# A hybrid encoder step: tokens normalized ahead of the input projection, convolutions that read PSUM, norms of queries and keys applied on load

## The chip, the cores and the metric

One core of a Trainium2 chip. The metric is the device time of one execution in microseconds. The engines are TensorE (PE, with PEld for its weight loads), VectorE (DVE), ScalarE (ACT), GpSimd (POOL) and SyncE (SP), which issues the DMAs.

## What is computed

One layer over 2048 prompt tokens (one request, zero states) and 8 x 16 sample tokens (with states), all in float32. Cut to what matters:

```python
h = rms_norm(x, norm_mix)                     # D_MODEL = 1024
p = h @ w_in                                  # 2056 columns GDN, 1824 columns RWKV
# gated delta rule: 4 heads of 128
qkv, gdn_conv_new = causal_dwconv(p_gdn[..., :1536], gdn_conv_buf, gdn_conv_w)   # 4 taps
q, k, v = split(silu(qkv))
q = l2_normalize(q) * 128 ** -0.5;  k = l2_normalize(k)
o_gdn, s_gdn_new = gdn_chunked(q, k, v, log_g, beta, s_gdn)
o_gdn = rms_norm(o_gdn, gdn_norm) * silu(z)
# RWKV-7: 8 heads of 64
ps, shift_new = causal_dwconv(p_rwkv, shift_buf, [rwkv_mu, 1 - rwkv_mu])         # 2 taps
kk = l2_normalize(kr * rwkv_k_k)
y, s_rwkv_new = rwkv7_recurrence(r, log_w, kr * (1 + (a - 1) * k_a), vr, -kk, kk * a, s_rwkv)
x = x + concat([o_gdn, o_rwkv]) @ w_out
# feed-forward of 2816 with a causal convolution of 3 taps in the gate
up = rms_norm(x, norm_ffn) @ w_up
gate, ffn_new = causal_dwconv(up[..., :2816], ffn_buf, ffn_conv_w)
x = x + (silu(gate) * up[..., 2816:]) @ w_down
y = rms_norm(x, norm_final)
```

The last rows before each convolution and the states are outputs too.

## The kernel before

Channels lie on partitions and tokens along the free dimension. The tokens go in five groups: 3, 4, 3, 3 blocks of 128, and 3 blocks with the 128 sample tokens behind them, so 384 or 512 columns. Each group has an input phase (`phase_in`) and an output phase (`phase_out`), in the order in0, in1, in2, out0, in3, out1, in4, out2, out3, out4.

Every projection is done in three passes (`mm3`): weight and input are each split into a rounded part and the rest (`split_w`, L419; `split_x`, L493). A block of 128 output channels is 24 products into one PSUM bank out of a ring of four (`psb`), which also serves the small products `psw`, `psa`, `psl`, `psbo`, `psgt` and `psn`. The scaling by 1/rms is left out of the inputs: the split takes x times the norm's weight, the sum of squares (`sumsq`) is made beside it, and 1/rms of each token (`g.rs`, tile `rsx`) is multiplied in as the bank is emptied.

That happens in `conv` (L506): POOL copies the history's last columns ahead of a tile `P` (L512), DVE writes bank times 1/rms into `P` (L513), POOL copies the new history out (L514), ACT multiplies with the last tap (L515), and DVE adds the other taps from shifted columns of `P` (L517). For the sample the same is done by segments (L521 to L527). The feed-forward's gate uses `conv` too.

`l2scale` (L616) runs four times per input phase, once for each GDN head and pair of RWKV heads. It sums squares on PE, takes Ln and Exp on ACT, stores the result to DRAM, loads it back spread over the partitions (`res<-l`, L632 and L635), multiplies q and k by it (L637) and stores them (`gd`). The direction of RWKV's keys waits for the same transfer (L764) before it is multiplied with the decays and stored (`rx`).

The two recurrences (`gdn_block` for 128 tokens and four heads, 17 of them; `rwkv_half` for 128 tokens and four heads, 34 of them) load these arrays (`gkq`, `rX`) and run beside the phases of other groups. Between their products stand long chains over DVE, ACT and POOL, with the inverse of triangular matrices (L788 to L837) the longest.

What sets the order: every part is a generator that yields the time its next operands are thought to take, and `drive` (L389) writes PE's order out from that, with the projections' products in the gaps of the recurrences. The order on the other engines comes from a planner that simulates the time. All DMAs are issued in order on SP's queue. The weights are loaded through four tiles `w32` and split by ACT (L425) and, by turns, POOL and DVE (L429).

Of the kernel before, what the change touches and what calls it, by code (L numbers as in the profile page):

```python
# [66 lines left out]
C_F32 = C_SI        # float32 up to here, masks behind  # L67
# [39 lines left out]
def pack_host(a):  # L107
    """Layout only: slices, transposes, zero padding."""
# [79 lines left out]
class Group:  # L188
    def __init__(self, t0, blocks, sample):
        self.t0, self.P, self.S = t0, blocks * 128, 128 if sample else 0  # L190
        self.nb, self.blk0 = blocks, t0 // 128
        self.n = self.P + self.S
        self.prep, self.tails, self.done, self.x = None, [], 0, None

    def seg(self, t):
        """the sample's part of a [p, tokens] AP, by request"""
        return t[:, self.P:self.n].rearrange("p (s t) -> p s t", t=SEG)


def bc(a, n):  # L200
    """a, along a new last axis"""
    return a.unsqueeze(len(a.shape)).to_broadcast(list(a.shape) + [n])


class Build:
# [7 lines left out]
    # ------------------------------------------------------------ set-up  # L213
    def setup(self, ctx):
# [14 lines left out]
        self.eps = cp.tile([128, 3], F32, name="eps")  # L229
        for i, v in enumerate((NEPS, LNEPS, 1.0)):  # L230
            nc.vector.memset(self.eps[:, i:i + 1], v)
# [32 lines left out]
        # constants by value  # L264
        self.mhalf = cp.tile([128, 1], F32, name="mhalf")
        nc.vector.memset(self.mhalf, -0.5)

        # parameters worked out once
# [8 lines left out]
        self.cw = der("cw", q("cw"), 0.5, own=True)           # half the taps: silu(y) = (1 + tanh(y/2)) y/2  # L277
# [6 lines left out]
        self.nhgn = der("nhgn", q("gn"), -0.5)  # L284
# [11 lines left out]
        # conv histories, and the sample's  # L296
# [12 lines left out]
        # per-token and per-block scalars  # L309
# [7 lines left out]
        # states: minus GDN's, and RWKV's with keys on partitions  # L317
# [4 lines left out]
        self.SB = [cp.tile([128, 2, 2, 64], F32, name=f"SB{i}") for i in range(2)]      # by pairs of heads, block-diagonal  # L322
# [3 lines left out]
        # scratch  # L326
        for i, g in enumerate(self.groups):
            d = lambda n, s: self.dp.tile(s, F32, name=f"{n}{i}")
            g.gd = d("gd", [4, 4, 128, g.n])        # k q v z, by head
            g.rx = [d(f"rx{j}_", [5, 128, g.n]) for j in range(4)]  # L330
            g.rh = d("rh", [8, 128, g.n])
            g.l2 = [d(f"l2{j}_", [6, g.n]) for j in range(4)]
# [6 lines left out]
    def a(self, g, name, dt=F32):  # L339
        """of the ring that the feed-forward's activations have in their phase"""  # L340
# [48 lines left out]
    def drive(self, main):  # L389
        """main to its end, then what is left of the tasks"""  # L390
# [18 lines left out]
    def load_w(self, src, tiles=KT):  # L409
        """[128, tiles * 128] of a weight, by [128, 512]"""  # L410
# [8 lines left out]
    def split_w(self, src, tiles=KT, ws=None):  # L419
        """a weight as pairs of [128, 512]: rounded, and what is left"""  # L420
# [12 lines left out]
    def mm3(self, ps, w, xs):  # L433
        """ps = sum over tiles of w^T x, both split: three passes"""
# [10 lines left out]
    def load_tok(self, g, t, a):  # L445
        """a group's tokens from [128, all tokens] of DRAM"""
# [9 lines left out]
    def pow_(self, out, in_):  # L456
        sh = list(in_.shape)
        e = self.mhalf
# [13 lines left out]
    def rms(self, g, acc):  # L472
        """in place: 1/rms of the channels whose squares acc sums by partition, on every partition"""
# [11 lines left out]
    def rsqrt(self, out, ps, scale=1.0):  # L485
        """(scale ps + eps)^-1/2"""
# [6 lines left out]
    def split_x(self, g, x, w=None):  # L493
        """x, times w of each channel: rounded, and what is left"""
# [10 lines left out]
    # ------------------------------------------------------------ causal convolution of a projected tile  # L505
    def conv(self, g, ps, rs, taps, hist, samp, out, rows=128):  # L506
# [4 lines left out]
        P = self.tp_.tile([128, 3 + 512], F32, tag="P", name="P", bufs=2)  # L511
        nc.gpsimd.tensor_copy(P[:, 0:h], hist)  # L512
        nc.vector.tensor_tensor(P[:, h:h + g.P], ps[:, 0:g.P], rs[:, 0:g.P], MUL)  # L513
        nc.gpsimd.tensor_copy(hist, P[:, g.P:g.P + h])  # L514
        nc.scalar.mul(out[r, 0:g.P], P[r, h:h + g.P], taps[-1][r])  # L515
        for i in range(h - 1, -1, -1):
            nc.vector.scalar_tensor_tensor(out[r, 0:g.P], P[r, i:i + g.P], taps[i][r], out[r, 0:g.P], op0=MUL, op1=ADD)  # L517
        S = None
        if g.S:
            S = self.tp_.tile([128, SEGS, 3 + SEG], F32, tag="PS", name="PS", bufs=1)  # L520
            nc.gpsimd.tensor_copy(S[:, :, 0:h], samp)  # L521
            nc.vector.tensor_tensor(S[:, :, h:h + SEG], g.seg(ps), g.seg(rs), MUL)
            nc.gpsimd.tensor_copy(samp, S[:, :, SEG:SEG + h])
            o = g.seg(out)
            nc.scalar.mul(o[r], S[r, :, h:h + SEG], taps[-1][r])
            for i in range(h - 1, -1, -1):
                nc.vector.scalar_tensor_tensor(o[r], S[r, :, i:i + SEG], taps[i][r], o[r], op0=MUL, op1=ADD)  # L527
        return P, S

    def shift(self, g, ps, i, out, rows=128):  # L530
        return self.conv(g, ps, g.rs, [self.q("mu")[:, i:i + 1], self.omu[:, i:i + 1]], self.hs[:, i:i + 1], self.ss[:, i, :].unsqueeze(2), out, rows)
# [4 lines left out]
    # ------------------------------------------------------------ input projection and all that is per token  # L536
    def phase_in(self, g):
        nc, q = self.nc, self.q
        xs = []
        g.rs = self.acc(g)  # L540
        ld = g.x or [self.load_x(g, k) for k in range(KT)]
        for k in range(KT):
            xs.append(self.split_x(g, ld[k], q("nm")[:, k:k + 1]))
            self.sumsq(g, g.rs, ld[k], k == 0)
        norm = self.spawn(self.late_rms(g, g.rs, 12000))
# [9 lines left out]
        # low-rank inputs  # L555
# [5 lines left out]
        self.shift(g, low[0], 0, la)  # L561
        nc.scalar.activation(la[0:64], la[0:64], AF.Tanh)
        sga = self.a(g, "sga")
        self.shift(g, low[1], 1, sga)
# [3 lines left out]
        P, S = self.shift(g, low[2], 2, sgb, 32)  # L568
        nc.scalar.activation(sgb[0:32], sgb[0:32], AF.Tanh, scale=0.5)
        nc.vector.tensor_scalar(sgb[0:32], sgb[0:32], 0.5, 0.5, op0=MUL, op1=ADD)  # L570
        self.spawn(self.gates(g, P, S))

        left = []
        for j in range(4):
            qk = []
            for a in range(2):
                ps = yield from block(15 + 4 * j + a)
                qk.append(self.prep_gdn(g, j, a, ps))
            left.append(self.spawn((yield from self.prep_rwkv(g, j, block, la, sga, sgb, qk))))
            for a in range(2, 4):  # L580
                ps = yield from block(15 + 4 * j + a)
                self.prep_gdn(g, j, a, ps)
        g.prep = left

    def gates(self, g, P, S):
        """beta and log decay of each token and GDN head, tokens on partitions"""
# [5 lines left out]
        for b in range(g.nb):  # L592
            self.tr(ps[:, 8 * b:8 * b + 8], P[64:72, 1 + 128 * b:129 + 128 * b], idn)
        if g.S:
            sm = self.t(g, "gth")[:, 0:128]
            nc.scalar.copy(sm[64:72].rearrange("p (s t) -> p s t", t=SEG), S[64:72, :, 1:17])
            self.tr(ps[:, 8 * g.nb:8 * g.nb + 8], sm[64:72], idn)
# [18 lines left out]
    def l2scale(self, g, j, qk, kk):  # L616
        """(sum of squares over a head's channels + eps)^-1/2 of RWKV's keys, GDN's queries and keys: the sums
        side by side in the array, 32 rows each, and the results spread over the partitions through DRAM"""
        nc = self.nc
        yield LB  # L620
        ps = self.psb(g, "psl")
        ss = (kk["s"], qk[0][1], qk[1][1])
        for n, s in enumerate(ss):
# [3 lines left out]
        nc.scalar.activation(rs[0:96], ps[0:96], AF.Ln, bias=self.eps[0:96, 0:1])  # L627
        nc.scalar.activation(rs[0:96], rs[0:96], AF.Exp, scale=-0.5)
        self.store(g.l2[j], rs[0:96:16])
        rk, rq, rK = [self.t(g, "res", 8) for _ in range(3)]  # L630
        for n in range(2):
            nc.sync.dma_start(rk[64 * n:64 * n + 64], g.l2[j][n:n + 1].to_broadcast([64, g.n]))  # L632
        kk["r"] = rk
        for n, r in enumerate((rq, rK)):
            nc.sync.dma_start(r, g.l2[j][2 + 2 * n:3 + 2 * n].to_broadcast([128, g.n]))  # L635
            y = qk[n][0]
# [677 lines left out]
```

## Time and profile before

| | |
|---|---|
| time of three runs | 3560.24, 3566.49, 3572.14 us |
| span of the profiled execution | 3558.0 us |
| PE, DVE, ACT, POOL busy | 95%, 67%, 42%, 52% |
| mean granted TensorE clock | 0.972 |
| DMA | 447.58 MB, mean 126 GB/s |

Of the profiled execution only the span from its first to its last instruction is known; it is 2.2 us under the fastest of the runs and 8.5 under their median. An engine's busy time counts its instructions, not the waits of its queue. A row of a group gives the line, engine, operation, out<-in, shapes and count, then busy time and mean ns of one, then the engine's idle time just before them and what ended it. A row of the timeline gives start and length in us and, in brackets, the idle time before it. A row of stretches gives the stretch, the busy time and count of each engine (PE, PEld, DVE, ACT, POOL), the granted clock, the DMA share and GB/s; its last row sums them.

### The profile page before, as it was taken

The numbers are of one execution on the slowest core, as the hardware profiler recorded it, in microseconds if no ns is written. First come the engines' busy times: TensorE is split into PE (matmuls) and PEld (weight loads), VectorE is DVE, ScalarE is ACT, GpSimd is POOL, SyncE is SP. The second block draws the span as 40 slices with busy tenths as digits, with TensorE's granted clock in tenths as the row PEclk, the third lists the DMA queues.
The fourth block names the chain that finished last, engine by engine and source line by source line (L and its number), as shares of the span: only waits on it lengthen the run. The fifth ranks groups of instructions, "written<-read, shape, count | busy, mean of one in ns | idle before, by whom it ended". The sixth has DMA issues, their size and how long they took to land. (4 is left out here: it accounts for less than half of the span.)

```text
span 3558.0 us, 60074 instructions
## 1 busy us (share of the span) xinstructions
PE 3372.0 (95%) x21661; PEld 2895.7 (81%) x21661; DVE 2376.5 (67%) x4277; ACT 1510.7 (42%) x2698; POOL 1833.0 (52%) x2335
## 2 busy tenths in 40 slices
PE   8989989999999989999999999899999999999997
PEld 7867768788999977777777767799979899988886
DVE  7777777786776677666655677776566665665444
ACT  5554344444333455443333455443324434453333
POOL 4545545655664544455454445566555355534442
PEclk9989999999999999999999999999999999999999
DMA  5534444453333344532222334533343433443322
GB/s 174 167 130 131 140 150 128 139 167 107 110 108 114 123 140 143 169 97 86 92 92 92 112 136 143 191 112 112 112 140 121 159 123 129 137 139 97 97 94 81
DMA packets 346265, 447.58 MB, mean 126 GB/s; under 512 B 30168, under 2 KB 194336, under 8 KB 345968
## 3 DMA queue, kind: packets, MB, share of 16 engines
q1 hardware_dynamic: 345968, 443.75, 38.9%
q8 instruction: 170, 2.79, 0.3%
q14 instruction: 127, 1.04, 0.1%
HBM read 372.60 MB, written 71.03 MB: 125 GB/s over the span
## 5 line engine op out<-in xcount | busy, mean ns | idle before, releaser
L425 ACT CAST whi<-w 128x512 fp32r<-128x512 f32 (+1 forms) x1070 | 651.2, 610 | 1115.7 <-PE psd L360 295.5
L429 POOL TENSOR_TENSOR wlo<-w,whi 128x512 fp32r<-128x512 f32 (+1 forms) x535 | 706.9, 1321 | 676.3 <-ACT whi L425 625.2
L360 PE MATMUL psi<-x,whi 128*128 128x384 f32 (+1 forms) x2480 | 737.7, 378 | 33.8 <-ACT x L501 14.0
L360 PEld LDWEIGHTS psi<-x,whi 128*128 128x128 f32 x2480 | 456.4, 196 | 96.2 <-issue 23.9
L360 PE MATMUL psup<-x,whi 128*128 128x384 f32 (+1 forms) x1760 | 504.3, 367 | 0.0
L360 PE MATMUL psga<-x,whi 128*128 128x384 f32 (+1 forms) x1760 | 502.6, 366 | 0.0
L429 DVE TENSOR_TENSOR wlo<-w,whi 128x512 fp32r<-128x512 f32 (+1 forms) x535 | 426.2, 797 | 77.0 <-ACT whi L425 76.8
L360 PE MATMUL psi<-x,wlo 128*128 128x384 f32 (+1 forms) x1240 | 456.2, 368 | 3.2 <-POOL wlo L429 3.1
L360 PEld LDWEIGHTS psga<-x,whi 128*128 128x128 f32 x1760 | 315.5, 189 | 28.1 <-issue 3.3
L360 PEld LDWEIGHTS psup<-x,whi 128*128 128x128 f32 x1760 | 316.4, 190 | 25.7 <-issue 1.8
L360 PE MATMUL psd<-ah,whi 128*128 128x384 f32 (+1 forms) x880 | 330.2, 375 | 7.0 <-ACT ah L1213 7.0
L360 PE MATMUL psd<-al,whi 128*128 128x384 f32 (+1 forms) x880 | 319.7, 363 | 4.5 <-POOL al L1215 4.5
L360 PE MATMUL psd<-ah,wlo 128*128 128x384 f32 (+1 forms) x880 | 318.7, 362 | 0.0
L360 PE MATMUL psup<-x,wlo 128*128 128x384 f32 (+1 forms) x880 | 316.6, 360 | 0.0
L360 PE MATMUL psga<-x,wlo 128*128 128x384 f32 (+1 forms) x880 | 315.3, 358 | 0.0
L1223 DVE TENSOR_TENSOR res<-res,psd 128x384 f32<-128x384 f32 (+1 forms) x240 | 145.3, 605 | 212.8 <-PE psd L360 212.1
L360 PEld LDWEIGHTS psi<-x,wlo 128*128 128x128 f32 x1240 | 241.7, 195 | 26.3 <-POOL wlo L429 5.0
L1215 POOL TENSOR_TENSOR al<-xin,ah 128x384 fp32r<-128x384 f32 (+1 forms) x110 | 126.0, 1146 | 144.4 <-ACT ah L1213 100.7
L513 DVE TENSOR_TENSOR P<-psga,rsx 128x384 f32<-128x384 f32 (+1 forms) x110 | 64.2, 584 | 197.7 <-PE psga L360 192.5
L360 PE MATMUL pso<-x,whi 128*128 128x384 f32 (+1 forms) x640 | 187.5, 373 | 8.9 <-DVE x L499 7.4
L360 PEld LDWEIGHTS psd<-ah,whi 128*128 128x128 f32 x880 | 167.3, 190 | 23.9 <-ACT ah L1213 8.5
L821 DVE TENSOR_TENSOR TUr<-TUr,pX 128x256 f16<-128x256 f16 x396 | 148.5, 412 | 53.2 <-PE pX L360 51.7
(342 smaller groups left out, 6753.4 us busy)
## 6 DMA issues: line engine op xcount, KB each, us to landing
w<-in_w_up SPq DMA_DIRECT2D x440, 256.0 KB
w<-in_w_in SPq DMA_DIRECT2D x310, 256.0 KB
w<-in_w_down SPq DMA_DIRECT2D x160, 256.0 KB
rX<-rx SPq DMA_DIRECT2D x68, 320.0 KB
w<-in_w_out SPq DMA_DIRECT2D x80, 256.0 KB
w<-in_w_down SPq DMA_DIRECT2D x80, 192.0 KB
rx<-res SPq DMA_DIRECT2D x48, 192.0 KB
gd<-res SPq DMA_DIRECT2D x48, 192.0 KB
```

The source lines that it names most:

```text
L360: self.nc.tensor.matmul(out, lhsT=lhsT, rhs=rhs, start=start, stop=stop)
L425: nc.scalar.copy(hi, w)
L429: eng.tensor_tensor(lo, w, hi.bitcast(F32), SUB)
L513: nc.vector.tensor_tensor(P[:, h:h + g.P], ps[:, 0:g.P], rs[:, 0:g.P], MUL)
L821: nc.vector.tensor_tensor(w, w, pX[:, y].rearrange("p u (n b) -> p u n b", b=b), ADD)
L1215: nc.gpsimd.tensor_tensor(lo, y, hi.bitcast(F32), SUB)
L1223: nc.vector.tensor_tensor(res[m], res[m], ps, ADD)
```

## The change

- Groups 1 to 4: a new task `norms`, started in the phase before, loads x a second time, sums the squares (ACT squares, POOL adds) and makes 1/rms. `phase_in` then multiplies x by weight and 1/rms in place on DVE before the split (ACT rounds, DVE takes the rest). Group 0 keeps the old way through `src`.
- `conv` reads its source directly: the PSUM bank in groups 1 to 4 of the input phases, a tile `P` in group 0 and in the feed-forward's gate. The tile with the history ahead is gone: the taps add to shifted columns of the output, the history comes in as a small addition of products made once per phase on POOL (`histories`), and ACT copies the new history out. The gate's logits are copied to SBUF by ACT for `gates`.
- `l2scale` is split: `l2sums`, per head, sums squares on PE, copies them out and stores them to DRAM; one `l2scale` at the phase's end loads all 24 rows, takes Ln and Exp once, and stores them. q and k are stored without their norm, RWKV's key direction too, multiplied with the decays straight away.
- The recurrences load the norms spread over the partitions and multiply: in `gdn_block` two broadcasts into the buffer of `kq` and `X *= kq`; in `rwkv_half`, for each of two pairs, two broadcasts into `rr` and one multiplication of two of the five arrays. The wait that the generator gives after the RWKV loads goes from 3000 to 3500.
- GDN's factor 128^-1/2 goes into the output's norm, `gdn_norm` from z into the output's gate; z then needs no ACT multiplication and no eviction of its own.

Comments and docstrings go too. The diff, cut:

```diff
+    def history(self, hist, taps, tmp):
...
+            nc.gpsimd.tensor_tensor(p, at(hist, n, h), wide(n, n, h), MUL)
...
+        nc.gpsimd.tensor_tensor(hist, hist, wide(0, 0, h), MUL)
...
+    def src(self, g, ps):
+        P = self.tp_.tile([128, 512], F32, tag="P", name="P", bufs=2)[:, 0:g.n]
+        self.nc.vector.tensor_tensor(P, ps, g.rs, MUL)
+        return P
+
+    def conv(self, g, src, taps, hist, samp, out, rows=128):
...
+        nc.scalar.mul(out[r], src[r], taps[-1][r])
+        S, o = (g.seg(src), g.seg(out)) if g.S else (None, None)
+        for i in range(1, h + 1):
+            t = taps[h - i][r]
+            nc.vector.scalar_tensor_tensor(out[r, i:g.P], src[r, 0:g.P - i], t, out[r, i:g.P], op0=MUL, op1=ADD)
+            if g.S:
+                nc.vector.scalar_tensor_tensor(o[r, :, i:SEG], S[r, :, 0:SEG - i], t, o[r, :, i:SEG], op0=MUL, op1=ADD)
+        if g.blk0:
+            nc.vector.tensor_tensor(out[r, 0:h], out[r, 0:h], hist[r], ADD)
+        nc.scalar.copy(hist, src[:, g.P - h:g.P])
         if g.S:
-            S = self.tp_.tile([128, SEGS, 3 + SEG], F32, tag="PS", name="PS", bufs=1)
...
+            nc.vector.tensor_tensor(o[r, :, 0:h], o[r, :, 0:h], samp[r], ADD)
+            nc.scalar.copy(samp, S[:, :, SEG - h:SEG])
...
+    def norms(self, g):
+        acc = self.acc(g)
+        for k in range(KT):
+            t = acc if k == 0 else self.t(g, "xin", NXI)
+            self.load_tok(g, t, self.I["x"][k])
+            yield 4000
+            nc.scalar.activation(t, t, AF.Square)
+            if k:
+                nc.gpsimd.tensor_tensor(acc, acc, t, ADD)
+        yield 8000
+        self.rms(g, acc)
+        g.rs = acc
...
     def phase_in(self, g):
...
+        if g.norm is None:
+            g.rs = self.acc(g)
...
+            norm = self.spawn(self.late_rms(g, g.rs, 12000))
+            src = lambda ps: self.src(g, ps)
+        else:
+            norm = g.norm
+            yield from self.until(norm)
+            for k in range(KT):
+                nc.vector.scalar_tensor_tensor(ld[k], ld[k], nm(k), g.rs, op0=MUL, op1=MUL)
+                xs.append(self.split_x(g, ld[k]))
+            src = lambda ps: ps
...
-    def l2scale(self, g, j, qk, kk):
+    def l2sums(self, g, j, squares):
         yield LB
         ps = self.psb(g, "psl")
...
+        self.nc.scalar.copy(rs[0:96], ps[0:96])
+        self.store(g.ssq[j], rs[0:96:16])
+
+    def l2scale(self, g, sums):
+        for t in sums:
+            yield from self.until(t)
+        yield 4000
+        rs = self.t(g, "grs")[0:24]
+        nc.sync.dma_start(rs, g.ssq.rearrange("j r t -> (j r) t"))
+        yield 4000
+        nc.scalar.activation(rs, rs, AF.Ln, bias=self.eps[0:24, 0:1])
+        nc.scalar.activation(rs, rs, AF.Exp, scale=-0.5)
+        self.store(g.l2.rearrange("j r t -> (j r) t"), rs)
...
     def gdn_block(self, g, i, samp=False):
...
+        kq = rp.tile([128, 4, 2, 128], F32, tag="gkq", name="gkqs", bufs=2)
+        for a in range(2):
+            nc.sync.dma_start(kq[:, :, a, :], g.l2[:, 4 - 2 * a, cols].unsqueeze(0).to_broadcast([128, 4, 128]))
...
+        nc.vector.tensor_tensor(X, X, kq, MUL)
...
     def rwkv_half(self, g, i, hf, samp=False):
...
+            rr = rp.tile([128, 128], F32, tag="rR", name="rR", bufs=2)
+            for e in range(2):
+                nc.sync.dma_start(rr[es[e]], g.l2[2 * hf + p, e:e + 1, cols].to_broadcast([64, 128]))
+            rr = rr.unsqueeze(1).to_broadcast([128, 2, 128])
+            nc.vector.tensor_tensor(x[:, 0:3:2, :], x[:, 0:3:2, :], rr, MUL)
+        yield 3500
...
     def main(self):
-        for kind, i in seq:
+        for n, (kind, i) in enumerate(seq):
+            if n + 1 < len(seq) and seq[n + 1][0] == "in":
+                g = G[seq[n + 1][1]]
+                g.norm = self.spawn(self.norms(g), 1)
```

More of the change, by code (lines that the diff above doesn't have):

```diff
@@ L331, in setup @@
             g.rh = d("rh", [8, 128, g.n])
-            g.l2 = [d(f"l2{j}_", [6, g.n]) for j in range(4)]
+            g.ssq = d("ssq", [4, 6, g.n])
+            g.l2 = d("l2", [4, 6, g.n])
             g.og = d("og", [8, 128, g.n])
@@ L503, in split_x, with histories @@
         return hi, lo
-    def conv(self, g, ps, rs, taps, hist, samp, out, rows=128):
+    def history(self, hist, taps, tmp):
+        nc = self.nc
+        h = hist.shape[-1]
+        ax = (slice(None),) * (len(hist.shape) - 1)
+        at = lambda t, a, b: t[ax + (slice(a, b),)]
+        wide = lambda n, a, b: taps[n].to_broadcast(list(at(hist, a, b).shape))
+        parts = []
+        for n in range(1, h):
+            p = tmp[n - 1][ax + (slice(0, h - n),)]
+            nc.gpsimd.tensor_tensor(p, at(hist, n, h), wide(n, n, h), MUL)
+            parts.append(p)
+        nc.gpsimd.tensor_tensor(hist, hist, wide(0, 0, h), MUL)
+        for n, p in enumerate(parts):
+            nc.gpsimd.tensor_tensor(at(hist, 0, h - n - 1), at(hist, 0, h - n - 1), p, ADD)
+    def histories(self, g, hist, samp, taps, h):
+        m = hist.shape[1]
+        if g.blk0:
+            tmp = self.t(g, "gth")
+            self.history(hist, taps, [tmp[:, 64 * n:64 * n + m * (h - 1)].rearrange("p (m h) -> p m h", h=h - 1) for n in range(h - 1)])
+        if g.S:
+            tmp = [self.t(g, "gth") for n in range(h - 1)]
+            tmp = [t[:, 0:m * SEGS * (h - 1)].rearrange("p (m s h) -> p m s h", s=SEGS, h=h - 1) for t in tmp]
+            self.history(samp, [t.unsqueeze(2) for t in taps], tmp)
+    def src(self, g, ps):
[3 more added lines that the diff above has]
+    def conv(self, g, src, taps, hist, samp, out, rows=128):
         nc = self.nc
@@ L510, in conv @@
         r = slice(0, rows)
[L511 to L517, printed above, removed]
@@ L567, in phase_in @@
         sgb = self.a(g, "sgb")
-        P, S = self.shift(g, low[2], 2, sgb, 32)
+        ls = src(low[2])
+        self.shift(g, ls, 2, sgb, 32)
         nc.scalar.activation(sgb[0:32], sgb[0:32], AF.Tanh, scale=0.5)
         nc.vector.tensor_scalar(sgb[0:32], sgb[0:32], 0.5, 0.5, op0=MUL, op1=ADD)
-        self.spawn(self.gates(g, P, S))
-        left = []
+        ba = self.t(g, "gth")
+        nc.scalar.copy(ba[64:72], ls[64:72])
+        self.spawn(self.gates(g, ba))
+        left, sums = [], []
         for j in range(4):
@@ L591, in gates @@
         ps = self.psr("psg")
[L592 to L597, printed above, removed]
+        for b in range(nb):
+            self.tr(ps[:, 8 * b:8 * b + 8], ba[64:72, 128 * b:128 * b + 128], idn)
         ba = self.rp.tile([128, 4, 8], F32, tag="gba", name="gba")
@@ L626, in l2scale, with prep_gdn @@
         rs = self.t(g, "grs")
[L627 to L636, printed above, removed]
-            nc.vector.scalar_tensor_tensor(y, y, (128.0 ** -0.5, 1.0)[n], r, op0=MUL, op1=MUL)
-            self.store(g.gd[j, 1 - n], y)
-        yield LR
-    def prep_gdn(self, g, h, a, ps):
+        self.nc.scalar.copy(rs[0:96], ps[0:96])
+        self.store(g.ssq[j], rs[0:96:16])
+    def l2scale(self, g, sums):
+        nc = self.nc
+        for t in sums:
[7 more added lines that the diff above has]
+        self.store(g.l2.rearrange("j r t -> (j r) t"), rs)
+    def prep_gdn(self, g, h, a, src):
         nc = self.nc
         if a == 3:
+            th = self.t(g, "gth")
+            nc.scalar.activation(th, src, AF.Tanh, scale=0.5)
             z = self.t(g, "res", 8)
-            nc.vector.tensor_tensor(z, ps, g.rs, MUL)
-            th = self.t(g, "gth")
-            nc.scalar.activation(th, z, AF.Tanh, scale=0.5)
-            nc.scalar.mul(z, z, self.nhgn)
-            nc.vector.scalar_tensor_tensor(z, th, 1.0, z, op0=ADD, op1=MUL)
+            nc.vector.scalar_tensor_tensor(z, th, 1.0, src, op0=ADD, op1=MUL)
             self.store(g.gd[h, 3], z)
@@ L654, in prep_gdn @@
         cw = self.cw[:, 4 * i:4 * i + 4]
-        self.conv(g, ps, g.rs, [cw[:, n:n + 1] for n in range(4)], self.hq[:, i, :], self.sq[:, i], y)
+        self.conv(g, src, [cw[:, n:n + 1] for n in range(4)], self.hq[:, i, :], self.sq[:, i], y)
         th = self.t(g, "gth")
@@ L658, in prep_gdn, with prep_rwkv @@
         nc.vector.scalar_tensor_tensor(y, th, 1.0, y, op0=ADD, op1=MUL)
-        if a == 2:
-            self.store(g.gd[h, 2], y)
-            return
-        s = self.t(g, "res", 8)
-        nc.scalar.activation(s, y, AF.Square)
-        return y, s
-    def prep_rwkv(self, g, j, block, la, sga, sgb, qk):
+        self.store(g.gd[h, (1, 0, 2)[a]], y)
+        if a < 2:
+            s = self.t(g, "res", 8)
+            nc.scalar.activation(s, y, AF.Square)
+            return s
+    def prep_rwkv(self, g, j, block, src, la, sga, sgb, qk, sums):
         nc, q = self.nc, self.q
@@ L722, in prep_rwkv @@
         kr = self.a(g, "rk")
-        self.shift(g, ps, 4 + 3 * j, kr)
-        kk = {"s": self.t(g, "res", 8)}
-        nc.scalar.activation(kk["s"], kr, AF.Square, scale=col(q("kk")))
-        kk["t"] = self.spawn(self.l2scale(g, j, qk, kk))
+        self.shift(g, src(ps), 4 + 3 * j, kr)
+        s = self.t(g, "res", 8)
+        nc.scalar.activation(s, kr, AF.Square, scale=col(q("kk")))
+        sums.append(self.spawn(self.l2sums(g, j, [s] + qk)))
         ps = yield from block(5 + 3 * j)
         v = self.a(g, "rv")
-        self.shift(g, ps, 5 + 3 * j, v)
+        self.shift(g, src(ps), 5 + 3 * j, v)
         def rest():
@@ L744, in rest @@
             self.store(rx[3], o)
+            o = self.t(g, "res", 8)
+            for tk, ex, *_ in parts:
+                nc.vector.scalar_tensor_tensor(tk(o), tk(kr), col(q("kk")), ex(ep, 0), op0=MUL, op1=MUL)
+            self.store(rx[0], o)
+            nc.vector.scalar_tensor_tensor(kr, th, 1.0, kr, op0=ADD, op1=MUL)
+            o = self.t(g, "res", 8)
+            for tk, ex, *_ in parts:
+                nc.vector.scalar_tensor_tensor(tk(o), tk(kr), col(self.hkk), ex(en, 1), op0=MUL, op1=MUL)
+            self.store(rx[2], o)
             nc.vector.scalar_tensor_tensor(r, r, col(q("rk")), kp, op0=MUL, op1=MUL)
@@ L759, in rest @@
             self.store(g.rh[2 * j + 1], bv)
-            while "r" not in kk:
-                yield 200
-            k = self.t(g, "gth")
-            nc.vector.scalar_tensor_tensor(k, kr, col(q("kk")), kk["r"], op0=MUL, op1=MUL)
-            o = self.t(g, "res", 8)
-            times(nc.gpsimd, o, k, ep, 0)
-            self.store(rx[0], o)
-            nc.vector.scalar_tensor_tensor(k, th, 1.0, k, op0=ADD, op1=MUL)
-            o = self.t(g, "res", 8)
-            for tk, ex, *_ in parts:
-                nc.vector.scalar_tensor_tensor(tk(o), tk(k), -0.5, ex(en, 1), op0=MUL, op1=MUL)
-            self.store(rx[2], o)
             yield LR // 2
@@ L1184, in phase_out @@
             self.sumsq(g, rs, res[m], m == 0)
+        g.rs = rs
         hs = [self.split_x(g, res[k], q("nf")[:, k:k + 1]) for k in range(KT)]
+        fw = self.fw.rearrange("p (m n) -> p m n", n=3)
+        self.histories(g, self.hf, self.sf, [fw[:, :, n:n + 1] for n in range(2)], 2)
         norm = self.spawn(self.late_rms(g, rs, 3000))
@@ L1190, in gate @@
             y = self.t(g, "xin", NXI)
-            self.conv(g, ps, rs, [self.fw[:, 3 * i + n:3 * i + n + 1] for n in range(3)], self.hf[:, i, :], self.sf[:, i], y)
+            self.conv(g, self.src(g, ps), [self.fw[:, 3 * i + n:3 * i + n + 1] for n in range(3)], self.hf[:, i, :], self.sf[:, i], y)
             th = self.t(g, "gth")
```

66 lines of the change are left out of this document (29 added, 37 removed).

## The prediction

> **What bounds the kernel now.** I read the page's busy times first, then the stretches by phase, then what stood ahead of TensorE's waits.
>
> ```profile
> span 3558.0 us, 60074 instructions
> PE 3372.0 (95%) x21661; PEld 2895.7 (81%) x21661; DVE 2376.5 (67%) x4277; ACT 1510.7 (42%) x2698; POOL 1833.0 (52%) x2335
> ```
>
> TensorE (PE) is busy 95%, and the change takes no product away. So all that can be gained is its idle time, 186 us. Where that lies is shown by the stretches: the first input phase, then the sums over the other four input phases and over the five output phases.
>
> ```profile
> 6.00:187.00 181.00, 157.97 (x802) 143.07 (x802) 137.22 (x203) 101.47 (x185) 86.23 (x123) 0.94 0.53 174
> sum 1045.00, PE 963.46 PEld 775.68 DVE 802.68 ACT 521.17 POOL 545.43; mean PE 240.86 PEld 193.92 DVE 200.67 ACT 130.29 POOL 136.36
> sum 2326.00, PE 2250.53 PEld 1976.95 DVE 1433.28 ACT 884.93 POOL 1199.78; mean PE 450.11 PEld 395.39 DVE 286.66 ACT 176.99 POOL 239.96
> ```
>
> Input phases 2 to 5: PE idle 81.5 of 1045 us (7.8%), VectorE (DVE) busy 76.8%. Output phases: 75.5 of 2326 (3.2%), DVE 61.6%. The first input phase adds 23 us. So DVE's answers come late where DVE is fullest; each point of DVE goes with 4.6/15.2 = 0.30% of PE idle. DVE also stands still there: groups by shape, then the timeline around the first and the last PE wait of one kind.
>
> ```profile
> L764 DVE SCALAR_TENSOR_TENSOR gth<-rk,par,res 128x384 f32<-128x384 f32 x12 | 8.4, 700 | 33.2 <-DMA res<-l 33.2
> L764 DVE SCALAR_TENSOR_TENSOR gth<-rk,par,res 128x512 f32<-128x512 f32 x8 | 6.0, 750 | 20.7 <-DMA res<-l 20.7
> L637 DVE SCALAR_TENSOR_TENSOR res<-res 128x384 f32<-128x384 f32 x24 | 18.8, 792 | 11.9 <-DMA res<-l 11.9
> L637 DVE SCALAR_TENSOR_TENSOR res<-res 128x512 f32<-128x512 f32 x16 | 14.1, 891 | 6.8 <-DMA res<-l 6.8
> ...
> 77.63 0.62 DVE L764 SCALAR_TENSOR_TENSOR gth<-rk,par,res 128x384 f32<-128x384 f32 x1 [3.79 <-DMA res<-l]
> 82.18 0.55 DVE L513 TENSOR_TENSOR P<-psi,rsx 128x384 f32<-128x384 f32 x1
> 82.88 0.59 PE L360 MATMUL psi<-x,whi 128*128 128x384 f32 x2 [3.08 <-DVE P L513]
> ...
> 1466.29 0.56 DVE L637 SCALAR_TENSOR_TENSOR res<-res 128x384 f32<-128x384 f32 x1 [3.58 <-DMA res<-l]
> 1469.18 0.79 PE L360 MATMUL pso<-x,whi 128*128 128x512 f32 x1 [5.04 <-DVE x L499]
> ```
>
> DVE waits 72.6 us for the spread norms (`res<-l`), with all that is queued behind it. At 82.88 PE wanted a bank that an eviction behind such a wait had not emptied; at 1469.18 a split input was late in the same way. Eleven PE waits over 0.6 us have such a DVE wait just ahead of them, 33.2 us in all, these two the first and the last.
>
> **The change, part by part**, against the span of 3558.0 us. The three runs took 3560.24 to 3572.14, their median is 8.5 above this span, and the prediction adds that 8.5.
>
> (a) *Norms out of the preparation.* The two scalings and the wait for the broadcasts leave the input phases. At most the 33.2 us go, at least nothing (DVE is 77% busy, another operation may stand in the place). The wait is directly ahead of the late operation in all eleven, so I take nearly all: -26.
>
> (b) *DVE work in input phases 2 to 5.* By line, summed over these four stretches: L513, L522, L645, L637, L470.
>
> ```profile
> sum 1045.00, DVE 62.90; mean DVE 15.72
> sum 1045.00, DVE 7.47; mean DVE 1.87
> sum 1045.00, DVE 8.60; mean DVE 2.15
> sum 1045.00, DVE 24.42; mean DVE 6.11
> sum 1045.00, DVE 20.49; mean DVE 5.12
> ```
>
> Multiplications by 1/rms, norm scalings and sums of squares go: 124 us. What replaces them is priced by these groups:
>
> ```profile
> L517 DVE SCALAR_TENSOR_TENSOR res<-P,par,res 128x384 f32<-128x384 f32 x144 | 114.1, 793 | 3.5 <-ACT res L515 1.5 <-ACT gw L609 0.2
> L758 DVE SCALAR_TENSOR_TENSOR grs<-grs,par,psgt 128x384 f32<-128x384 f32 x12 | 7.3, 605 | 0.0
> L502 DVE SCALAR_TENSOR_TENSOR x<-x,par 128x384 fp32r<-128x384 f32 x24 | 15.7, 679 | 0.2 <-ACT x L501 0.2
> L502 DVE SCALAR_TENSOR_TENSOR x<-x,par 128x512 fp32r<-128x512 f32 x16 | 13.0, 830 | 2.5 <-ACT x L501 2.5
> L614 DVE TENSOR_TENSOR lgl<-lg,lgh 128x16 fp32r<-128x16 f32 x2 | 0.3, 166 | 0.0
> L964 DVE TENSOR_TENSOR gon<-po,gs 128x512 f32<-128x512 f32 x17 | 11.7, 686 | 3.0 <-POOL gs L461 2.5
> L1086 DVE TENSOR_TENSOR ryc<-pY,rs 128x256 f32<-128x256 f32 x34 | 14.2, 417 | 1.0 <-ACT rs L1084 0.8
> ```
>
> Taps that read PSUM: 108 of 128x384 at L758's 0.605 instead of 0.793, -20. Normalizing x: 16 x 0.679 + 16 x 0.830 = +24. History adds: 27 x 4 and 27 for the sample at L614's 0.166 = +22. Recurrences that lie in these stretches: 6 of 17 GDN blocks at 2 x 0.686 = +8, 12 of 34 RWKV halves at 2 x 0.417 = +10. Net -80 of 802.7 us, 7.7 points, by 0.30% of 1045 us each: -24. The 19 us that (a) empties here can't go twice, so 62/81.5 of it: -18 (0 to -24).
>
> [...]
>
> (c) *POOL and ACT.* The copies around `P` go: L512 and L514 over the whole span.
>
> ```profile
> sum 3558.00, POOL 78.07; mean POOL 78.07
> sum 3558.00, POOL 101.74; mean POOL 101.74
> ...
> L1195 POOL TENSOR_TENSOR xin<-xin,rsx 128x384 f32<-128x384 f32 x66 | 69.4, 1052 | 14.9 <-DVE xin L1194 13.6
> ```
>
> 180 us of POOL go and 28 adds of the early sums of squares come, 30 us at 1.05. POOL is 52% busy and seldom last before PE: -3 (0 to -10; if POOL were the bound, most of the 150). ACT: 15 of the 20 pairs of Ln and Exp with their table loads go (L627 and L628 over the span), three quarters of 72 us, and some 294 small history copies come, at L1084's price 60 us. About even, and hidden by ACT's 58% of idle time:
>
> ```profile
> sum 3558.00, ACT 38.04; mean ACT 38.04
> sum 3558.00, ACT 34.40; mean ACT 34.40
> ...
> L1084 ACT ACTIVATE rs<-rs 128x4 f32<-128x4 f32 x34 | 6.9, 203 | 67.9 <-DVE rs L1083 67.9
> ```
>
> (d) *PSUM banks held longer.*
>
> ```profile
> 52.85 0.51 PE L360 MATMUL psi<-x,whi 128*128 128x384 f32 x2
> ...
> 54.93 0.51 PE L360 MATMUL psi<-x,whi 128*128 128x384 f32 x2
> ```
>
> Twelve products start between these two, 0.173 us apart, so a block of 24 at 384 tokens takes 4.2 us. In phases 2 to 5 a bank is free after one ACT multiply, three taps of 0.605 (one for a shift) and a small copy, instead of one eviction (0.55 at 82.18): some 2.5 to 3 us longer, more when DVE is behind. The ring has four banks; `psw` and `psa` take two of them right after a block. So a key block's bank must be free within one block and a bit. 32 key and value blocks: none late gives 0; all late as at 82.88, by 3.08, gives +99. The first input phase has such waits only behind (a)'s waits, so I stay near the lower end: +8.
>
> (e) *Norms applied on load.* 17 `X *= kq` and 68 `x *= rr` each wait on DVE for a transfer; evictions, half of the weights' `wlo` and the other recurrence's inverse are queued behind them.
>
> ```profile
> PE pA L360 <- DMA rX<-rx: 4.2, 2, 2.4
> ...
> L360 PE MATMUL pA<-rX x544: 375/376/792, 209.5 to 2843.3; 64*128 64x256 f32 x182
> L1016 SPq DMA_DIRECT2D rX<-rx x68: 359/377/1207, 87.0 to 2784.4; - x68
> L632 SPq DMA_DIRECT2D res<-l x40: 445/488/1344, 74.1 to 2271.9; - x40
> ...
> 3127.03 0.64 PE L360 MATMUL pso<-x,whi 128*128 128x512 f32 x2
> ```
>
> Only 2 of 68 loads of `rX` were late for PE, so the lower end is 0. If the first of each half and each block waits as L764 did (53.9/20 = 2.7 us) and PE loses as much of it as in (a) (33.2/72.6 = 0.46): 51 x 2.7 x 0.46 = +63. Here one transfer is waited for and not a store and a load in a chain: near the lower end, +8. On SP's queue 136 broadcasts of `rr`, 34 of `kq` and 36 loads of x come in and 80 go: some 126 x 0.488 = 61 us more over the span, behind which weight loads stand; hidden by the loads' run ahead of PE, else up to +28 by the same 0.46. The later start of a group's recurrence is hidden: they end shortly after 2843 (`pA`), the last output phase begins at 3127.
>
> (f) *Phase starts.* Input phases 2 to 5 get one more operation (0.679) ahead of each first split: 4 x 0.68 to 4 x 8 x 0.68, +3 to +22; the early norm helps there: +4.
>
> (g) *Output phases.* DVE gains 110 history adds (18 us), 11 blocks (15) and 22 halves (18): 51 us, 2.2 points, 0 to +15 by the slope; these phases have room: +8.
>
> Sum: -26 - 18 - 3 + 8 + 8 + 4 + 8 = -19, so 3539 us of span and **3547 us** of time.
>
> **Rivals.** Change that a measurement of this kernel can tell: 0.3%, 11 us.
>
> *The wait only moves* (slower). (e) at its upper end with the rest as summed: 3547 - 8 + 63 = 3602; halfway 3571. For it: L764 shows that a load with a consumer close behind it on DVE lands late. Against: PE's own waits for `rX`. Above 19 us more than I allow, 27 us in all, or 1.15 us for each of the 51, it decides.
>
> *Banks* (slower). (d) at half its upper end: 3547 - 8 + 50 = 3589. For it: 82.88, where one late eviction stopped PE. Against: most key blocks in phases 2 to 5 run with recurrences between them, which stretches the ring. [...]
>
> *The input phases become like the output phases* (a larger gain): idle from 104 us in all five (8.5% of 1226) to 3.2%, 39 us: -65. With (e) and (g) as taken 3566 - 65 + 16 = 3517, without them and with (c)'s 10, 3491. For it: the slope of 0.30% may be steeper near a full queue. Against: 69% is still above 61.6%.
>
> *Nothing moves*: DVE was late only where order makes PE wait: 3560 to 3570.
>
> **How the numbers follow.** My sum 0.50 (its own range 3525 to 3570; 0.40 of it faster, 0.10 within 0.3%), like the output phases 0.14, nothing 0.08, the moved wait 0.18, banks 0.10. So faster 0.54, same 0.18, slower 0.28. The range: from 3480, a little under the largest gain, to 3605, which takes in the moved wait's upper end and leaves out the banks' upper half.
>
> **What would show it.** (a) No DVE wait for `res<-l`; PE waits like 82.88 gone. (b) DVE under 71% in input phases 2 to 5, taps near 605 ns. (d) PE waits of `psi`, `psa` or `psgt` that an L517-like tap or an ACT copy ends. (e) DVE idle ahead of the multiplications by `rr` and `kq`: under 1 us each. (f) PE waits for `x` at phase starts under 3 us. Wrong I am if (d) or (e) shows tens of us, or if input phases keep 7% idle with DVE at 70%.

## The result, and the profile after

The changed kernel takes 3598.2 us (median of four runs, 3596.2 to 3602.3), the kernel before on the same chip 3564.8 us (four runs, 3560.2 to 3572.1). The ratio is 1.0098, 95% interval 1.0083 to 1.0113: slower by 33 us where 3547 us, 19 us faster, were forecast. The profiled execution took 3599.95 us.

The page's first lines, and the sums over input phases 2 to 5 and over the output phases, for the changed kernel:

```profile
span 3598.1 us, 60064 instructions
PE 3374.8 (94%) x21661; PEld 2896.0 (80%) x21661; DVE 2352.5 (65%) x4403; ACT 1459.9 (41%) x2887; POOL 1674.8 (47%) x1796
```

```profile
sum 1039.00, PE 956.56 PEld 770.74 DVE 730.97 ACT 451.97 POOL 458.91; mean PE 239.14 PEld 192.69 DVE 182.74 ACT 112.99 POOL 114.73
sum 2380.00, PE 2258.34 PEld 1981.82 DVE 1483.95 ACT 903.11 POOL 1137.86; mean PE 451.67 PEld 396.36 DVE 296.79 ACT 180.62 POOL 227.57
```

VectorE, ScalarE and GpSimd all have less to do. TensorE's idle time still grew from 186 to 223 us: hardly in the input phases (81.5 to 82.4 us), but in the output phases from 75.5 to 121.7 us. What DVE waited for, in two rows of its waits (who waited for whom; total us, times, longest):

```profile
DVE gkq L913 <- DMA gkqs<-l: 69.6, 15, 9.6
DVE rX L1073 <- DMA rX<-rx: 58.5, 51, 2.9
```

L913 is `X *= kq` in `gdn_block`, L1073 is `x *= rr` in `rwkv_half`. The 72.6 us of waits for `res<-l` are gone, and 128 us stand in their place. The timeline and the stretches around one of them show what such a wait does:

```profile
521.87 1.23 DVE L913 TENSOR_TENSOR gkq<-gkq,gkqs 128x1024 f32<-128x1024 f32 x1 [9.60 <-DMA gkqs<-l]
...
524.67 0.26 PE L358 MATMUL pP<-TUr,Nhr 128*128 128x128 f16 x1 [7.51 <-DVE TUr L869]
...
527.93 0.84 PE L358 MATMUL psi<-x,whi 128*128 128x384 f32 x2
...
531.21 0.51 PE L358 MATMUL psi<-x,whi 128*128 128x384 f32 x2
```

```profile
524.70:526.00 1.30, 1.30 (x13) 1.30 (x12) 0.81 (x2) 1.19 (x3) 0.00 (x0) 0.50 0.72 222
526.00:528.00 2.00, 2.00 (x9) 2.00 (x8) 1.42 (x4) 0.54 (x2) 0.00 (x0) 0.50 0.65 228
528.00:530.00 2.00, 2.00 (x10) 1.70 (x9) 0.00 (x0) 0.23 (x2) 0.00 (x0) 0.54 0.07 25
530.00:532.00 2.00, 2.00 (x16) 2.00 (x14) 1.71 (x3) 0.43 (x1) 1.29 (x1) 1.00 0.00 0
```

DVE stood 9.6 us; a step of the other recurrence's inverse (`TUr`) was queued behind it, and TensorE stood 7.5 us. Then TensorE's granted clock (the third column from the right) was 0.50 to 0.54 until 530 and 1.00 from there to 532, and two `psi` products took 0.84 us at 527.93 and 0.51 us at 531.21. So this long wait is paid for twice.

### The profile page after: what moved, and what is told of

Same layout as the page of the kernel before. It is cut to its first block, busy times and chain, and to the rows that moved or that the text cites. A ratio compares the mean times of both kernels' runs of the same rounds, so it can differ in the third digit from the quotient of the medians.

```text
span 3598.1 us, 60064 instructions
## 1 busy us (share of the span) xinstructions
PE 3374.8 (94%) x21661; PEld 2896.0 (80%) x21661; DVE 2352.5 (65%) x4403; ACT 1459.9 (41%) x2887; POOL 1674.8 (47%) x1796
## 5 line engine op out<-in xcount | busy, mean ns | idle before, releaser
L358 PE MATMUL psi<-x,whi 128*128 128x384 f32 (+1 forms) x2480 | 728.5, 375 | 23.1 <-DVE x L497 8.6
L427 DVE TENSOR_TENSOR wlo<-w,whi 128x512 fp32r<-128x512 f32 (+1 forms) x535 | 418.6, 783 | 104.8 <-ACT whi L423 104.2
L845 POOL MEMSET Rr<- 128x512 f16 x198 | 103.9, 526 | 183.8 <-PE pX L358 131.5
```

The costliest lines, as they stand in the source:

```text
L358: self.nc.tensor.matmul(out, lhsT=lhsT, rhs=rhs, start=start, stop=stop)
L427: eng.tensor_tensor(lo, w, hi.bitcast(F32), SUB)
L845: nc.gpsimd.memset(R, 0.0)
```

## The experiments

Theory T, formed from this trace: the wait has moved onto DVE's queue; the load of the GDN norms lands late, and what costs the time is the queue behind the multiplication that waits for it. The later runs call it Q, against the rival C, that the block's own chain is late by the load. The other rivals: the added DVE work itself (R1), the early normalization and the convolutions from PSUM (R2), the issue of so many transfers (R3). Each time below is a median; the kernel before took 3562 to 3566 us beside them.

**Which load.** Constants in place of the loads:

```diff
-            nc.sync.dma_start(kq[:, :, a, :], g.l2[:, 4 - 2 * a, cols].unsqueeze(0).to_broadcast([128, 4, 128]))
...
-        nc.vector.tensor_tensor(X, X, kq, MUL)
+        nc.vector.tensor_tensor(X, X, self.eps[:, 1:2].unsqueeze(2).unsqueeze(3).to_broadcast([128, 4, 2, 128]), MUL)
...
```

> The changed kernel with the 34 broadcast loads of the GDN norms (gkqs<-l) left out; X is multiplied by a constant from SBUF instead, so that all 34 multiplications stay and only the load and the wait for it go (the values are not those of the reference). Theory T, the wait moved onto DVE's queue: DVE's 69.6 us of wait ahead of the kq multiplication go, and with them about 58 us of TensorE waits that stand right behind them; some of that falls back on the X load: 3555 us (3535 to 3575). Theory R1, the added DVE work itself costs: within 10 us of 3598. Theory R2, the loss is from the early normalization and from the convolutions that read PSUM: within 10 us of 3598.

> The changed kernel with the 136 broadcast loads of the RWKV norms (rR<-l) left out, the multiplication of x[0] and x[2] by a constant from SBUF kept (the values are not those of the reference). T: DVE waits here mostly for rX itself (58.5 us against 4.9 us for rR), and the kernel before waited for rX as well (53.9 us), so little goes: 3588 us (3578 to 3598). R1 and R2: within 10 us of 3598. R3, the issue of 136 more transfers on SP (581 ns each, 79 us) delays all loads: 3560 us or less, and DVE's wait for gkqs<-l falls below 50 us.

> Both of the above: the changed kernel without any load of norms in the recurrences, all multiplications on load kept, by a constant (the values are not those of the reference). T: 3545 us (3525 to 3570), TensorE idle in the output phases back from 122 us to near the 76 us of the kernel before. R1: above 3585, TensorE idle in the output phases stays above 105 us. R2: above 3585 too, with the loss at the ends and starts of phases. R3: lower than the kernel with the kq loads alone left out by more than 20 us.

Measured: 3541.8 us without the GDN norms' load, 3597.4 without the RWKV norms' load, 3539.5 without both. So taking away the 34 loads of `gkqs` gave 56 us, and taking away the 136 of `rR` nothing. R1 and R3 fall: all the multiplications are still there in the first, and 136 issues less on SP's queue (561 ns each in the median in the changed kernel) moved nothing in the second. The 53.9 us that the second expectation gives to `rX` in the kernel before are DVE's wait of L764 for `res<-l`; no DVE instruction waited for `rX` there. DVE's waits in the kernel without the `gkqs` loads:

```profile
DVE rX L1071 <- DMA rX<-rx: 58.4, 53, 3.3
DVE gkq L910 <- DMA gkq<-gd: 34.5, 15, 4.4
```

The 58 us of short waits for `rX` stand there as before. No run takes them away, so what they cost is not known. The wait ahead of `X *= kq` fell by 35 us, and the time by 56. What is left of it is for X and stands elsewhere: without the norms to wait for, the multiplication comes right behind X's own load (at 231.8 us in the second block, which the changed kernel multiplies at 303.6). So this run takes away the load and its wait and moves the multiplication too; the tied runs below tell these apart. Its page and the granted clocks:

```profile
span 3548.4 us, 59969 instructions
PE 3360.4 (95%) x21661; PEld 2886.4 (81%) x21661; DVE 2355.9 (66%) x4403; ACT 1460.6 (41%) x2887; POOL 1679.8 (47%) x1796
```

```profile
core 0: 3548.4 us, clock 0.975
```

```profile
core 0: 3598.1 us, clock 0.967
```

The last is the changed kernel. Of the 49.7 us between the two profiled spans, 35.3 are idle time of TensorE and 14.4 its busy time: the same products, at a higher clock.

**Norms back in the preparation.** `l2scale` per head and the scalings as in the kernel before; the rest of the change stays.

```diff
-        sums.append(self.spawn(self.l2sums(g, j, [s] + qk)))
+        kk["t"] = self.spawn(self.l2scale(g, j, qk, kk))
...
-        nc.vector.tensor_tensor(X, X, kq, MUL)
...
-            nc.vector.tensor_tensor(x[:, 0:3:2, :], x[:, 0:3:2, :], rr, MUL)
...
```

> The changed kernel with the norms of queries and keys as in the kernel before: worked out head by head in the preparation and multiplied there, nothing multiplied on load. The early normalization of the tokens and the convolutions that read PSUM stay. T: the output phases return to the times of before, the input phases give back part of their gain (the 33 us of DVE's wait for l2 come back): 3550 us (3530 to 3575). R1: the same, 3545 us. R2: 3590 us or more, since what costs is still there.

Measured: 3569.8 us, near the upper end of T; R2 falls too. DVE waits for the spread norms as in the kernel before:

```profile
DVE gth L812 <- DMA res<-l: 42.9, 14, 4.0
...
DVE res L688 <- DMA res<-l: 25.4, 16, 5.0
```

Against the 3539.5 us without any load of norms, taking the norms out of the preparation is worth 30 us.

**Why the load is late and slow.** The norms go into one of two buffers, which the last output products of the block before (`po`) still read. In 11 of the 13 blocks that come right behind another one, the load is issued within 0.2 us of the end of these products; X's own loads are issued 47 us or more ahead of the multiplication. One block, and the wait of the issue for `po` over the kernel:

```profile
605.00 0.39 PE L358 MATMUL po<-SN,gkqs 128*128 128x128 f32 x2
...
605.41 0.93 SPq L900 DMA_DIRECT2D gkqs<-l  x2
...
615.57 1.23 DVE L913 TENSOR_TENSOR gkq<-gkq,gkqs 128x1024 f32<-128x1024 f32 x1 [7.58 <-DMA gkqs<-l]
```

```profile
SPq L900 <- PE po L358: 14.1, 9, 3.5
```

So little hides the load, and most of its length becomes DVE's wait. No run gave the norms a buffer of their own, so what an earlier issue would bring is open. The next two runs change its length. From the issue of its second transfer to use the load took 8.6 to 10.2 us in the groups of 512 tokens, and 4.6 to 5.3 in the others wherever DVE waited for it.

```diff
-            g.l2 = d("l2", [4, 6, g.n])
+            g.l2 = d("l2", [4, 6, g.n + 32])[:, :, 0:g.n]
```

> The changed kernel with each row of the norms in DRAM lengthened by 32 tokens (128 B) that nothing uses; nothing else differs. The load of the GDN norms took 4.6 to 5.3 us from issue to use in the groups of 384 tokens (rows of 1536 B) and 8.6 to 10.2 us in the groups of 512 (rows of 2048 B). Theory A, the length of the row makes the difference (128 partitions read the same few rows, and rows 2048 B apart get in each other's way): all loads 4.5 to 5.5 us, DVE's wait for gkqs<-l falls from 69.6 to about 32 us, time 3565 to 3578 us. Theory B, the load is late for another reason in these groups (its buffer, the queue, other transfers): loads and time as before, 3593 to 3603 us.

```diff
+            g.lkq = d("lkq", [g.n // 128, 4, 2, 128])
...
+        nc.sync.dma_start(kq, g.lkq[i].unsqueeze(0).to_broadcast([128, 4, 2, 128]))
```

> The changed kernel with the GDN norms stored a second time, block by block ([block, head, key or query, token]), so that a block's load is one transfer of 4096 B to each partition in place of two with eight pieces of 512 B. A: fewer and longer pieces, load to use about 3 to 4 us, the wait nearly gone: 3545 us (3538 to 3560). B: 3590 to 3603 us.

Measured: 3560.6 us with rows longer by 128 bytes, just below theory A's range, and 3548.6 us (ratio to before 0.996, 0.9946 to 0.9974) with the norms stored block by block. All DMA traffic while the same load is under way, as stretches of the changed kernel and of the one with longer rows (last columns: DMA share, GB/s):

```profile
606.50:613.00 6.50, 6.50 (x57) 6.36 (x57) 1.49 (x5) 0.92 (x2) 3.04 (x3) 1.00 0.34 68
```

```profile
604.50:607.50 3.00, 3.00 (x37) 2.87 (x36) 1.33 (x5) 0.30 (x1) 2.29 (x3) 1.00 0.67 153
```

68 against 153 GB/s, with the DMA engines two thirds idle in the slow one: 128 partitions read the same few rows 2048 bytes apart, and with 128 bytes more between them the rate in these stretches more than doubles. Why it does, the runs don't show. DVE's wait for the load with longer rows, and with contiguous blocks:

```profile
DVE gkq L913 <- DMA gkqs<-l: 38.1, 15, 6.3
```

```profile
DVE gkq L915 <- DMA gkqs<-lkq: 25.6, 14, 3.3
```

Theory A held, B fell; the wait with longer rows is 38.1 us where some 32 were expected, and the contiguous load still took 3.6 to 7.0 us from issue to use, longer than I expected.

**Queue or chain.** First the multiplications issued later in the program:

```diff
-        yield 3000
-        nc.vector.tensor_tensor(X, X, kq, MUL)
+        yield 2500
         pE = self.psr("pE")
...
+        yield 5000
+        nc.vector.tensor_tensor(X, X, kq, MUL)
+        yield 1300
...
```

> The changed kernel with the loads as they are, and the multiplications issued later: X times the norms behind the decays, 7.5 us of other products after the load's issue in place of 3; x times the norms 3.5 us after its load's issue in place of directly behind it. T, DVE's queue stands behind a multiplication whose load is in flight: the wait of 69.6 us falls to 10 to 25 us and rX's 58.5 us to below 15 us, DVE does other work meanwhile: 3545 us (3530 to 3565). Rival, the recurrence's own chain sets the time, and whatever is put off there is late by as much: 3590 to 3620 us.

Measured: 3601.3 us. The rival's number came, but not for its reason; the waits are what they were:

```profile
DVE gkq L936 <- DMA gkqs<-l: 68.1, 15, 7.1
DVE rX L1077 <- DMA rX<-rx: 55.8, 55, 3.0
```

In VectorE's instruction order, in the same 13 blocks, the multiplication stood 1 to 4 places behind the previous block's state update (`SN`) in the changed kernel, and 2 to 5 here: the planner, which sets this order, put it nearly where it was. So this run tells nothing between Q and C. Next, the multiplication on GpSimd (`nc.gpsimd.tensor_tensor(X, X, kq, MUL)`), with the slow and with the contiguous load:

> The changed kernel with the multiplication of X by the GDN norms on GpSimd in place of VectorE (17 instructions, about 2.46 us each there by the nearest row, against 1.2 to 1.3 us), loads as they are. Theory Q, the loss is that DVE's queue stands behind the wait: DVE no longer waits for gkqs<-l, 3565 us (3550 to 3580). Theory C, the loss is that the block's own products come later by the load: 3595 to 3610 us. Theory P, GpSimd's queue stands in DVE's place, and the weights' low parts that it makes come late: 3610 us or more, with TensorE waits that end with POOL wlo.

> The kernel with the GDN norms stored block by block (3548.6 us), and besides the multiplication of X on GpSimd. Theory Q: DVE's remaining 25.6 us of wait go, 3538 us (3530 to 3546). C and P: 3546 to 3565 us, since GpSimd's multiplication is longer by 1.2 us in each of 17 blocks and waits as long.

Measured: 3614.0 us, in P's range, and 3581.7 us, above every range given. DVE no longer waits for the load, but GpSimd does, and the two products that the block's decays start from (`lm`) stand behind the multiplication there. In the first of the two, GpSimd's wait and what ended TensorE's longest waits:

```profile
POOL gkq L913 <- DMA gkqs<-l: 37.3, 9, 9.9
```

```profile
PE pE L358 <- POOL lm L908: 46.2, 18, 9.0
```

The same row of the changed kernel:

```profile
PE pE L358 <- POOL lm L908: 0.2, 1, 0.2
```

In VectorE's queue and in GpSimd's alike the wait held up something that TensorE needs, in the second for 46.2 us of TensorE's waits; but for P I had named the weights' low parts, and it was `lm`. It took a dependency to move the multiplication: its scalar operand is a column of ones made from the decays' product.

```diff
-        nc.vector.tensor_tensor(X, X, kq, MUL)
...
+        nc.scalar.activation(one, pd[:, 0:1], AF.Identity, scale=0.0, bias=self.eps[:, 2:3])
...
+        yield 3000
+        nc.vector.scalar_tensor_tensor(X, X, one, kq, op0=MUL, op1=MUL)
+        yield 1500
```

> The changed kernel, loads as they are, with the multiplication of X by the norms tied to the block's decays: its scalar operand is a column of ones that ScalarE derives from the decays' product, so that VectorE's queue has it 3 to 11 places behind the previous block's gon, and no longer directly behind the state update. Theory Q, the loss is what stands behind the wait in VectorE's queue: the wait for gkqs<-l falls from 69.6 to below 30 us, time 3565 us (3550 to 3580). Theory C, the loss is the block's own chain: X comes as late as before or later, 3595 to 3620 us.

> The same tie, with the norms stored block by block (3548.6 us without the tie). Q: the remaining 25.6 us of wait go, 3540 us (3530 to 3548). C: 3548 to 3570 us.

Measured: 3537.7 us with the slow load kept, ratio to before 0.9927 (0.9905 to 0.995); 3517.8 us with the contiguous load, 0.9875 (0.9848 to 0.9902), the best version here, 80 us under the changed kernel. It now stands 8 to 12 places behind the state update in the same 13 blocks. DVE's waits there with the slow load:

```profile
DVE gkq L939 <- ACT ged L932: 22.1, 8, 8.0
...
DVE gkq L939 <- DMA gkqs<-l: 5.6, 2, 4.7
```

DVE's idle time ahead of the multiplication fell from 72.9 to 35.0 us. The load is as it was (the two blocks that still wait for it use it 9.4 and 9.5 us after the issue of its second transfer), and in every block more time passes from the load's issue to the multiplication than in the changed kernel; yet 60 us went: Q holds, C falls. The edit also adds waits to the generator, and so changes TensorE's order; the run with 5000 and 1300 in the same place gained nothing, so these are not the 60 us. Both times lie below Q's ranges. Why the gain exceeds Q's price was not found. The page of the best version:

```profile
span 3513.5 us, 60059 instructions
PE 3342.1 (95%) x21661; PEld 2869.6 (82%) x21661; DVE 2369.8 (67%) x4403; ACT 1464.5 (42%) x2904; POOL 1700.8 (48%) x1796
```

Against the kernel before, TensorE is idle 14.6 us less (171.4) and busy 29.9 us less, at a granted clock of 0.980 in place of 0.972.

**The other parts.** The early normalization taken out of the kernel without loads of norms:

```diff
-                g.norm = self.spawn(self.norms(g), 1)
+                g.norm = None
```

> The kernel without any load of norms in the recurrences (constants in their place, the values are not those of the reference; 3539.5 us), and besides without the tokens' norms worked out ahead of the input phases: they are worked out as in the first group, in the phase, and the convolutions read a normalized copy in SBUF. If the early normalization is what makes the input phases shorter (16 us in the fourth, 12 in the third of them after an output phase): 3565 us (3555 to 3580). If it costs the ends of the output phases as much as it gains: 3540 us (3533 to 3548).

Measured: 3564.5 us, so early normalization, with the convolutions from PSUM that go with it, is worth 25 us there. Two more, both on the contiguous load:

> The kernel with the GDN norms stored block by block (3548.6 us), with the history steps of the feed-forward's convolution left out (the products ahead of the phase, the additions to the first two columns and the copies of the last two; the values of the first columns are not those of the reference). If these small instructions (110 additions of about 263 ns on DVE, 110 copies on ACT) are why the second and the fourth output phase are 8 and 12 us longer than in the kernel before: 3530 us (3522 to 3540). If not: 3542 to 3553 us.

> The kernel with the GDN norms stored block by block (3548.6 us), and the normalization of x at the start of an input phase (8 instructions of 605 ns on DVE in each of four phases) moved to GpSimd. If these stand ahead of the last activations of the output phase before and cause the waits of TensorE for ah (19.1 us in five places): 3540 us (3533 to 3546). If GpSimd's own work there (al) is then late instead: 3546 to 3560 us.

Measured: 3546.9 and 3547.8 us, no difference that counts from 3548.6. With x normalized on GpSimd, TensorE's waits for `ah` fell little and those for `al` grew. Before that, and with it:

```profile
PE psd L359 <- ACT ah L1274: 19.1, 5, 7.4
...
PE psd L359 <- POOL al L1276: 6.9, 5, 2.3
```

```profile
PE psd L359 <- ACT ah L1274: 16.3, 5, 5.7
...
PE psd L359 <- POOL al L1276: 12.9, 5, 4.8
```

## Why the prediction was wrong, point by point

**(e) failed**, the norms applied on load: +8, where taking away the load of the GDN norms alone gave 56 us. I took the value near the lower end because TensorE had waited for 2 of 68 loads of `rX` only, and because "one transfer is waited for and not a store and a load in a chain". Both reasons failed. TensorE's wait for `rX` stood in its own queue and came to 4.2 us in all; a wait on DVE held up what was queued behind it there: at 521.87, 9.6 us on DVE became 7.5 us on TensorE. And the norms' load is not like `rX`: it is a broadcast from a few rows, as only `res<-l` was in the kernel before, the row I set aside, and its buffer lets it be issued only 5 to 11 us ahead of its use. The factor from DVE's wait to time was wrong as well: I took 0.46, from waits of 3 us, where 35 us less of waits of up to 9.6 us gave 56 us, more than a quarter of it as busy time of TensorE. The rival *the wait only moves* had named the mechanism and the place, and its sum came close, 3602 against 3598. The closeness is partly luck: it took 51 waits of 2.7 us at 0.46, and 2.7 us is what they were on average (136.4 us by the groups of L913 and L1073), but the 17 of GDN at a much higher factor account for all that a run has shown.

```profile
L1073 DVE TENSOR_TENSOR rX<-rX,rR 128x256 f32<-128x256 f32 x68 | 35.8, 527 | 63.5 <-DMA rX<-rx 58.5 <-DMA rR<-l 4.9
L913 DVE TENSOR_TENSOR gkq<-gkq,gkqs 128x1024 f32<-128x1024 f32 x17 | 25.5, 1501 | 72.9 <-DMA gkqs<-l 69.6 <-issue 3.2
```

**The rest of the sum held in its total, in part by luck.** Without (e) it said 3539; the kernel without the loads took 3539.5. Its sums over input phases 2 to 5 and the output phases:

```profile
sum 1015.00, PE 948.24 PEld 766.03 DVE 730.73 ACT 450.56 POOL 461.20; mean PE 237.06 PEld 191.51 DVE 182.68 ACT 112.64 POOL 115.30
sum 2339.00, PE 2244.28 PEld 1970.81 DVE 1486.98 ACT 905.19 POOL 1144.54; mean PE 448.86 PEld 394.16 DVE 297.40 ACT 181.04 POOL 228.91
```

The input phases fell from 1045 to 1015 us; (a) to (d) and (f) said -35, all of it idle time of TensorE. Only half came from there (81.5 to 66.8 us); the other half is TensorE's busy time (963 to 948 us for about as many products), which the prediction held fixed. (a) The wait for `res<-l` is gone, and with the early normalization in place the norms in the preparation cost 30 us against 26; without it, the kernel that has them taken out gained nothing (3564.5 us). (b) DVE was at 70.4% of the input phases in the changed kernel, under the 71% forecast, and the taps that read PSUM took 610 ns. That TensorE's idle time falls with DVE's share by a fixed slope was not tested by itself: in the changed kernel it did not fall (82.4 us at 70.4%), which was one of the prediction's own signs of being wrong. New work was priced too low: the multiplications on load took 61 us of DVE where 51 were summed, and an addition of the history on two columns 280 ns where 166 were taken.

```profile
L547 DVE SCALAR_TENSOR_TENSOR res<-psi,par,res 128x383 f32<-128x383 f32 x36 | 22.0, 610 | 1.5 <-ACT res L543 1.4
```

(c) GpSimd lost 158 us of work, and nothing shows that it mattered by itself. (d) The banks were not a cost. TensorE's waits in the changed kernel that a copy out of a bank ends:

```profile
PE psgt L358 <- ACT grs L680: 1.1, 1, 1.1
PE psi L358 <- ACT hq L552: 0.5, 1, 0.5
```

(f) was probably sized too small. TensorE's waits for the last activations of an output phase grew from 11.5 to 25.7 us, where I had +4 for the phase starts. That the multiplications of x on DVE ahead of these activations are the cause is not shown: on GpSimd they left 16.3 of 19.1 us of the waits for `ah`. In the kernel before, then in the changed one:

```profile
PE psd L360 <- ACT ah L1213: 7.0, 5, 2.1
PE psd L360 <- POOL al L1215: 4.5, 5, 1.1
```

```profile
PE psd L358 <- ACT ah L1272: 18.7, 5, 7.3
...
PE psd L358 <- POOL al L1274: 7.0, 5, 2.4
```

(g) The output phases lengthened by 13 us without the loads (2326 to 2339), against +8; leaving out the gate's history steps changed the time by no more than 2 us.

Open: the early normalization alone (3569.8 us) and the batched norms alone (3564.5, without their loads) each leave the time within 6 us of before, and both together take 25 us off it. So the terms do not add up one by one as the prediction had them. The first still has the waits for `res<-l`; why the second gains nothing by itself was not found.

## What to carry to other kernels

Before an operation is moved onto a load, look at what stands behind it in its engine's queue, at what holds the load's buffer and so how early it can be issued, and at the longest wait that this leaves: here 70 us of waits up to 9.6 us cost some 56. Price a transfer by one of its own pattern; for the broadcast from a few rows here the layout in DRAM decided the rate (68 against 153 GB/s in the stretches shown). Where a planner orders the queues, a later line in the program moved the multiplication by hardly a place; a dependency moved it, and turned a loss of 33 us into a gain of 24 with the slow load untouched.

## What the runs showed of the hardware that was not expected

While rows 2048 bytes apart were read by all 128 partitions in pieces of 512 bytes, DMA moved 68 GB/s in the stretch shown; with 128 bytes more between the rows, 153 GB/s. And after a stall of 7.5 us TensorE's next five microseconds ran at a granted clock of 0.50 to 0.54, two products taking 0.84 us where two of the same shape took 0.51 us at 1.00, so that part of what this stall cost shows as busy time. Over the whole kernel the same 21661 products took 3374.8 us in the changed kernel, at a mean clock of 0.967, and 3342.1 us in the best one, at 0.980.
